# Score and broadcast matmuls of a four-branch decoder trunk on 64 rows of the array, or on 128 rows with zeros

## The chip, the cores and the metric

The kernel runs on one core of one Trainium2 chip. The metric is the device time of one execution in microseconds (us). TensorE (PE in the profile; its weight loads have a row of their own, PEld) multiplies, VectorE (DVE), ScalarE (ACT) and GpSimd (POOL) do the rest, and SyncE (SP) issues the weight transfers.

## The reference, cut to what matters

Two layers, 256 tokens, width 2048. Each layer projects the normed input once and feeds four mixers, whose gated outputs are merged, projected and added to the input. The three matmuls that the change touches come from these lines:

```python
# D, latent attention: 8 heads, key of 128 plain + 64 rotary columns (the rotary key is shared by all heads)
q_full = jnp.concatenate([q[..., :MLA_NOPE], q_rope], axis=-1)
k_full = jnp.concatenate([kv[..., :MLA_NOPE], broadcast(k_rope)], axis=-1)
logits = jnp.einsum('bhqd,bhkd->bhqk', q_blk, k) * scale
# B, forgetting attention (FoX): 16 heads of 64 columns
logits = logits + fq[..., :, None] - log_f_cum[..., None, :]
# A, SSD: 16 heads; decay between two tokens from the cumulative sum of one row per head
seg = a_cum[:, :, :, None] - a_cum[:, :, None, :]
```

## The kernel before, in words

Every large product is computed from split operands: a weight piece of 512 KB comes in by DMA (`fetch`, L152), ACT rounds it to `hi`, DVE forms the remainder `lo`, and PE adds three products (`chunk_a` L163: 512 columns a matmul; `chunk_b` L184: 256 columns). Weight pieces stream through five `raw` buffers and three pairs of `hi`/`lo`. Each layer goes through the in-projections of D, C, A and B, with the mixer of the branch before running in the background: a generator on the list `bg`, advanced by one step (`step`) after each piece. A scheduler of the framework then sets the order of each engine's instructions, so that small matmuls of a mixer stand one by one between the three-product groups of the stream.

The small matmuls of this text are:

- Latent attention, `attention` (L244) with `terms` of D (L498): for each head and each of two query blocks, one matmul of 128 rows on `kn` and one of 64 rows on `krope`, for odd heads on rows 64 to 127 (L257). `S_D` is the PSUM tile of the scores.
- FoX, the same function with `fterms` (L784): per head a bias matmul of 128 rows on `fR` (L254, 384 columns) and two score matmuls of 64 rows on `fk` (L257). `S_B` is the tile. Even heads lie on rows 0 to 63, odd ones on rows 64 to 127.
- SSD, `ssd_gen` (L687): per head one matmul of 64 rows (L721) that spreads the head's row of `aR` over all partitions, into `rb`.

Scores on `krope` and `fk` are plain fp32 and leave two records each, two passes over the columns; the `rb` and `fR` matmuls are in the rounded type of the stream and leave one. The transposes of the probabilities (`pt_B`, `pt_D`, L283) and the products of the GLA branch (`gla_o`, L637) are also plain fp32, on 128 rows.

Of the kernel before, what the change touches and what calls it, by code (L numbers as in the profile page):

```python
# [18 lines left out]
P = 128  # L19
# [18 lines left out]
def trunk(ctx: ExitStack, tc: tile.TileContext, x, pos, vecs, rows, dskip, pre, post, glaw2,  # L38
# [25 lines left out]

# [1 line left out]
    xt = [slot(i, f"x0_{i}") for i in range(2)]  # L66
# [32 lines left out]

# [1 line left out]
    cos = cp.tile([P, T], F32, tag="cos", name="cos")  # L101
# [33 lines left out]

# [1 line left out]
    bg = []  # L137
# [25 lines left out]
    def chunk_a(src, p0, nk, xh, xl, k0, name, groups=None, own=None):  # L163
        """acc[token, 512 columns] over nk row blocks; within a group of pieces the first 128 tokens go first"""
        acc = acc_tile(name)
        a2 = [acc[:, 0], acc[:, 1]]
        if own:
            a2[1] = ps.tile([P, 2, 512], F32, tag="s", name=name + "_1")[:, 0]
        kp = 0
        for n in groups or [1] * (nk // 2):  # L170
            w = [fetch(src[p0 + kp + i], own=own[i] if own and n > 1 else None) for i in range(n)]
            ks = [(2 * kp + i, w[i // 2], slice((i % 2) * 512, (i % 2 + 1) * 512)) for i in range(2 * n)]
            order = ([(tt, k) for k in ks for tt in range(2)] if n == 1 else
                     [(tt, k) for tt in range(2) for k in ks])
            for tt, (k, (hi, lo), c) in order:
                ts_ = slice(tt * P, (tt + 1) * P)
                PE.matmul(a2[tt], xh[:, k0 + k, ts_], hi[:, c], start=(k == 0), stop=False)  # L177
                PE.matmul(a2[tt], xh[:, k0 + k, ts_], lo[:, c], start=False, stop=False)  # L178
                PE.matmul(a2[tt], xl[:, k0 + k, ts_], hi[:, c], start=False, stop=(k == nk - 1))  # L179
            kp += n  # L180
            step(n)
        return a2 if own else acc
# [29 lines left out]
    def transpose_split(src, nb, dh, dl, d0, scale, name):  # L212
        """src(tt, b) -> [P, P] token-major block; dh/dl[:, d0 + b, :] feature-major."""
        for b2 in range(nb // 2):
            pt = psT(f"tr_{name}{b2}").rearrange("p (a t) -> p a t", a=2)
            for j in range(2):
                for tt in range(2):
                    PE.transpose(pt[:, j, tt * P:(tt + 1) * P], src(tt, 2 * b2 + j), ident)
            d = slice(d0 + 2 * b2, d0 + 2 * b2 + 2)
            if scale is None:  # L220
                S.copy(dh[:, d], pt)
                V.tensor_tensor(dl[:, d], pt, dh[:, d].bitcast(F32), ALU.subtract)
            else:
                for j in range(2):
                    S.activation(dh[:, d0 + 2 * b2 + j], pt[:, j], AF.Copy, scale=scale(2 * b2 + j))
                for j in range(2):
                    b = 2 * b2 + j
                    V.scalar_tensor_tensor(dl[:, d0 + b], pt[:, j], scale(b), dh[:, d0 + b].bitcast(F32),
                                           ALU.mult, ALU.subtract)
            yield  # L230
# [7 lines left out]
    def silu_gate(acc, dst, name):  # L238
        """dst = silu(acc), both [P, 2, 512]"""
        S.activation(dst, acc, AF.Sigmoid)  # L240
        V.tensor_tensor(dst, acc, dst, ALU.mult)

# [1 line left out]
    def attention(npair, dv, scale, terms, bias, v, gate, name):  # L244
# [58 lines left out]

# [1 line left out]
    def norm_x(tt, src, dst, ssq, prow):  # L305
        """hh, hl of 128 tokens from src [P, 2048] and the sums of squares of its parts"""
        tot = small([P, 1], f"xtot{tt}")
# [38 lines left out]
    for l in range(DEPTH):  # L346
# [7 lines left out]

# [1 line left out]
        cc = slot(5, "cc").rearrange("p (a b t) -> p a b t", a=2, b=2)  # L356
# [14 lines left out]
        drain()  # L371
# [1 line left out]
        accs = acc_tile("acc_small")[:, 0, :T]  # L373
        for kh in range(2):
            hi, lo = fetch(w_sm[l, kh], 896)
            for k8 in range(8):
# [4 lines left out]
                PE.matmul(accs[:112], lo[:, c], hh[:, k], start=False, stop=(k == 15))  # L381
        krope = small([P, T], "krope", bufs=1)
        krr = small([P, T], "krr", bufs=1)
        for o in (0, 64):
            S.copy(krope[o:o + 64], accs[0:64])
            S.copy(krr[o:o + 32], accs[32:64])
            S.copy(krr[o + 32:o + 64], accs[0:32])
        raw2 = slot(6, "raw2")
        lr, gw2 = raw2[:16, 0:T], raw2[:16, 512:1024]
# [6 lines left out]
        def gates_gen(l=l, krr=krr, krope=krope, lr=lr, gw2=gw2):  # L396
# [17 lines left out]
            yield  # L414
            # cumulative sums: per 128 tokens (SSD), over all (FoX)
            ca, cf, ce = mxz, zz, e
# [18 lines left out]
            V.tensor_tensor(krr, krr, sin, ALU.mult)  # L435
            V.tensor_tensor(krope, krope, krr, ALU.add)
            yield
            # low-rank gate operands: all four products of the halves stacked along the rows
            for dst, src in ((lrs, lr), (gs, gw2)):
# [9 lines left out]
        gs = small([112, 512], "gs", F32R, bufs=1)  # L449
        aR = small([64, T], "aR", F32R, bufs=1)  # L450
        fR = small([P, 3 * P], "fR", F32R, bufs=1)
# [37 lines left out]

        def mla_gen(l=l, qr=qr, qn=qn, kn=kn, dv_=dv_, lgate=lgate, krope=krope, oh=oh, ol=ol):  # L490
            for o, t in ((0, cos), (4, sin)):
                V.tensor_tensor(qr[:, o:o + 4], qr[:, o:o + 4],
                                t.rearrange("p (o n) -> p o n", o=1).to_broadcast([P, 4, T]), ALU.mult)
            V.tensor_tensor(qr[:, 0:4], qr[:, 0:4], qr[:, 4:8], ALU.add)
            yield

            def terms(h):
                s_ = slice(64 * (h % 2), 64 * (h % 2) + 64)  # L498
                return [(qn[:, h], kn[:, h]), (qr[s_, h // 2], krope[s_])]

            yield from attention(4, 128, 192 ** -0.5, terms, None, dv_, lgate, "D")
            noh = st.tile([P, 8, T], F32R, tag="oh", name="oD_h")
            nol = st.tile([P, 8, T], F32R, tag="ol", name="oD_l")
            res["D"] = (noh, nol)
            yield from transpose_split(lambda tt, b: lgate[:, tt, b * P:(b + 1) * P], 8, noh, nol, 0, None, "oD")
# [4 lines left out]

# [1 line left out]
        gqk = slot(5, "gqk").rearrange("p (s h t) -> p s h t", s=2, h=4)  # L512
# [15 lines left out]

# [1 line left out]
        mixed = sl.tile([P, 2, 2048], F32, tag="mixed", name="mixed")  # L530
# [15 lines left out]

# [1 line left out]
        def gla_gen(l=l, gqk=gqk, gv=gv, gg=gg, lrs=lrs, gs=gs):  # L548
# [113 lines left out]

# [1 line left out]
        xsT = slot(3, "xsT").rearrange("p (a t) -> p a t", a=8)  # L664
# [20 lines left out]

# [1 line left out]
        def ssd_gen(l=l, xsT=xsT, bcT=bcT, zg=zg, aR=aR, tokg=tokg):  # L687
# [26 lines left out]
            for g in range(2):  # L714
                yp = ps.tile([P, 2, 512], F32, tag="s", name=f"y{g}")
                late = []
                for hg in range(8):
                    h = 8 * g + hg
                    pr = psT(f"rb{h}")
                    sel = id2[:64, h:h + 1].to_broadcast([64, P])  # L720
                    PE.matmul(pr[:, 0:T], sel, aR, start=True, stop=True)  # L721
# [40 lines left out]

# [1 line left out]
        fq = slot(5, "fq").rearrange("p (a t) -> p a t", a=8)  # L764
        fk = slot(6, "fk").rearrange("p (a t) -> p a t", a=8)
        for dst in (fq, fk):
            for c in range(2):
                acc = chunk_b(w_in[l], nxt(8), 4, hh, hl, "acc_f")
                if c == 0:
                    S.copy(dst[:, 4 * c:4 * c + 4], acc)  # L770
                else:
                    V.tensor_copy(dst[:, 4 * c:4 * c + 4], acc)
        fv = slot(7, "fv").rearrange("p (a b) -> p a b", a=2)
# [9 lines left out]

        def fterms(h, fq=fq, fk=fk):  # L784
            s_ = slice(64 * (h % 2), 64 * (h % 2) + 64)
            return [(fq[s_, h // 2], fk[s_, h // 2])]

# [10 lines left out]

# [1 line left out]
        mh0 = st.tile([P, 8, T], F32R, tag="oh", name="m_h0")  # L800
# [63 lines left out]

# [1 line left out]
def _a(w):  # L866
    """[K, 512 n] -> pieces [n * K / 256, 128, 1024], two blocks of 128 rows by 512 columns each"""
    K, N = w.shape
# [3 lines left out]
def _b(w):  # L872
    """[2048, 128 n] -> pieces [2 n, 128, 1024], eight blocks of 128 rows by 128 columns each"""
    N = w.shape[1]
    return (w.reshape(2, 8, P, N // P, P).transpose(3, 0, 2, 1, 4).reshape(-1, P, 1024))


def _b4(w):
    """[512, 256 n] -> pieces [n, 128, 1024]: two column blocks by four row blocks"""
    N = w.shape[1]  # L880
# [71 lines left out]
```

## Time and profile before

| | |
|---|---|
| median of 3 runs | 2628.51 us (2628.07 to 2629.09) |
| profiled execution: span from first to last instruction | 2626.6 us |
| mean granted clock of TensorE, as a share | 0.997 |
| PE busy | 2594.7 us, 99% |
| DVE, ACT, POOL busy | 58%, 48%, 1% |
| HBM read | 455.02 MB, 175 GB/s over the span |

No other time is listed for the profiled execution than its span; the median stands 1.9 us above it. PE's records end after the next one has begun, so what a matmul costs is read from the starts: from the last matmul of the stream ahead of it to the second one behind it, less the stream's own pace for two.

### The profile page before, as it was taken

What the parts mean: (1) busy time and instruction counts of PE and PEld (TensorE: products, weight loads), DVE (VectorE), ACT (ScalarE), POOL (GpSimd) and SP (SyncE); (2) the same over time, 40 slices, a digit from 0 to 9 for tenths busy, and PEclk for the clock granted to TensorE, in tenths of its full rate; (3) what the DMA queues carried; (4) which work ended last, traced back from release to release, by engine and by line L of the source; (5) the groups of instructions that cost most, each with busy time, mean ns of one, the idle gap of its engine ahead of it and who ended that gap; (6) DMA issues with size and microseconds to landing.
All of it is one profiled execution on the core that took longest, in us unless ns stands there. A gap on an engine that the chain in (4) does not pass through costs nothing.

```text
span 2626.6 us, 34754 instructions
## 1 busy us (share of the span) xinstructions
PE 2594.7 (99%) x13810; PEld 2203.6 (84%) x13810; DVE 1527.4 (58%) x1880; ACT 1247.9 (48%) x1587; POOL 17.4 (1%) x28
## 2 busy tenths in 40 slices
PE   8999999999999999999999999999999999999998
PEld 6898888988899787888878888889888987788887
DVE  6755854676654455555556558546766544555554
ACT  5644544455444444444455445444554444444443
POOL 0000000000000000000000000000000000000000
PEclk9999999999999999999999999999999999999999
DMA  6544545555555554655655445555545555446554
GB/s 227 184 153 143 162 167 185 184 193 168 169 194 176 168 169 141 218 189 182 213 160 185 145 137 176 169 181 183 174 168 184 185 173 169 164 159 206 188 183 153
DMA packets 126722, 461.48 MB, mean 176 GB/s; under 512 B 14656, under 2 KB 15168, under 8 KB 125664
## 3 DMA queue, kind: packets, MB, share of 16 engines
q1 hardware_dynamic: 126144, 459.11, 53.0%
q8 instruction: 108, 1.77, 0.3%
q14 instruction: 54, 0.44, 0.0%
q10 hardware_dynamic: 416, 0.17, 0.0%
HBM read 455.02 MB, written 4.19 MB: 175 GB/s over the span
## 4 chain that ended last, share of the span: by engine, by line
PE 97%; DVE 1%; ACT 1%; issue 0%; DMA 0%; POOL 0%; SPq 0%; DVEq 0%; POOLq 0%; ACTq 0%
PE acc_mC L178 2%; PE acc_f L194 2%; PE acc_f L193 2%; PE acc_f L192 2%; PE acc_mA L177 2%; PE acc_mD L178 2%; PE acc_mA L178 2%; PE acc_mC L177 2%; PE acc_mD L177 2%; PE acc_mA L179 2%; PE acc_mC L179 2%; PE acc_mD L179 2%; PE acc_mB L178 2%; PE acc_mB L177 2%; PE acc_mB L179 2%; PE acc_y L179 2%
## 5 line engine op out<-in xcount | busy, mean ns | idle before, releaser
L157 DVE TENSOR_TENSOR lo<-raw,hi 128x1024 fp32r<-128x1024 f32 x842 | 1027.5, 1222 | 870.6 <-ACT hi L156 869.2
L156 ACT CAST hi<-raw 128x1024 fp32r<-128x1024 f32 x842 | 882.2, 1050 | 1128.2 <-PE acc_f L193 109.7
L194 PE MATMUL acc_f<-hh,lo 128*128 128x256 f32 x512 | 145.1, 283 | 0.0
L193 PE MATMUL acc_f<-hl,hi 128*128 128x256 f32 x512 | 144.9, 283 | 0.0
L192 PE MATMUL acc_f<-hh,hi 128*128 128x256 f32 x512 | 144.9, 283 | 0.0
L194 PE MATMUL acc_x<-hh,lo 128*128 128x256 f32 x384 | 108.8, 283 | 0.0
L193 PE MATMUL acc_x<-hl,hi 128*128 128x256 f32 x384 | 108.7, 283 | 0.0
L192 PE MATMUL acc_x<-hh,hi 128*128 128x256 f32 x384 | 108.7, 283 | 0.0
L178 PE MATMUL acc_mC<-lo,hh 128*128 128x512 f32 x256 | 104.9, 410 | 0.0
L178 PE MATMUL acc_mD<-lo,hh 128*128 128x512 f32 x256 | 103.1, 403 | 0.0
L178 PE MATMUL acc_mA<-lo,hh 128*128 128x512 f32 x256 | 102.5, 400 | 0.0
L177 PE MATMUL acc_mA<-hi,hh 128*128 128x512 f32 x256 | 101.4, 396 | 0.0
L177 PE MATMUL acc_mC<-hi,hh 128*128 128x512 f32 x256 | 100.5, 393 | 0.0
L178 PE MATMUL acc_mB<-lo,hh 128*128 128x512 f32 x256 | 100.2, 391 | 0.0
L179 PE MATMUL acc_mA<-hi,hl 128*128 128x512 f32 x256 | 100.0, 391 | 0.0
L177 PE MATMUL acc_mD<-hi,hh 128*128 128x512 f32 x256 | 100.0, 391 | 0.0
L179 PE MATMUL acc_mD<-hi,hl 128*128 128x512 f32 x256 | 99.8, 390 | 0.0
L179 PE MATMUL acc_mC<-hi,hl 128*128 128x512 f32 x256 | 99.8, 390 | 0.0
L179 PE MATMUL acc_mB<-hi,hl 128*128 128x512 f32 x256 | 99.7, 389 | 0.0
L177 PE MATMUL acc_mB<-hi,hh 128*128 128x512 f32 x256 | 99.6, 389 | 0.0
L192 PEld LDWEIGHTS acc_f<-hh,hi 128*128 128x128 f32 x512 | 98.3, 192 | 0.1
L193 PEld LDWEIGHTS acc_f<-hl,hi 128*128 128x128 f32 x512 | 98.3, 192 | 0.1
(415 smaller groups left out, 6028.3 us busy)
## 6 DMA issues: line engine op xcount, KB each, us to landing
raw<-in_w_in_dram SPq DMA_DIRECT2D x624, 512.0 KB, 3.4
raw<-in_w_br_dram SPq DMA_DIRECT2D x128, 512.0 KB, 3.4
raw<-in_w_out_dram SPq DMA_DIRECT2D x64, 512.0 KB, 3.3
raw<-in_w_ukv_dram SPq DMA_DIRECT2D x16, 512.0 KB, 4.3
raw<-in_w_uq_dram SPq DMA_DIRECT2D x12, 512.0 KB, 3.3
x<-in_x_dram SPq DMA_DIRECT2D x4, 512.0 KB, 5.7
xr<-in_x_dram SPq DMA_DIRECT2D x2, 1024.0 KB, 7.1
pn<-in_post_dram SPq DMA_DIRECT2D x2, 1024.0 KB, 7.4
```

What stands on the lines that cost most here:

```text
L156: S.copy(hi[:, :n], raw[:, :n])
L157: V.tensor_tensor(lo[:, :n], raw[:, :n], hi[:, :n].bitcast(F32), ALU.subtract)
L177: PE.matmul(a2[tt], xh[:, k0 + k, ts_], hi[:, c], start=(k == 0), stop=False)
L178: PE.matmul(a2[tt], xh[:, k0 + k, ts_], lo[:, c], start=False, stop=False)
L179: PE.matmul(a2[tt], xl[:, k0 + k, ts_], hi[:, c], start=False, stop=(k == nk - 1))
L192: PE.matmul(acc[:, b], hi[:, c], xh[:, k], start=(k == 0), stop=False)
L193: PE.matmul(acc[:, b], hi[:, c], xl[:, k], start=False, stop=False)
L194: PE.matmul(acc[:, b], lo[:, c], xh[:, k], start=False, stop=(k == 15))
```

## The change

The rotary key is written into a tile `kr2` with two halves: the rows of the even heads and zeros, and zeros and the rows of the odd heads. `fk` becomes `fk0` and `fk1` in the same manner, `aR` gets 64 more rows of zeros, and the three matmuls use all 128 rows. `krope` and `krr` move into `raw2`, in slot 6. `fk1` takes slot 4, where the row of the next layer's norm (`prow`) is loaded later. The zeros are written by POOL (`kr2` once, `fk0` and `fk1` in each layer) and by DVE (`aR`). Comments are dropped too.

```diff
+    kr2 = cp.tile([P, 2, T], F32, tag="kr2", name="kr2")
+    G.memset(kr2, 0.0)
...
-        krope = small([P, T], "krope", bufs=1)
-        krr = small([P, T], "krr", bufs=1)
+        raw2 = slot(6, "raw2")
+        krope, krr = raw2[:, 1024:1024 + T], raw2[:, 1280:1280 + T]
...
-            V.tensor_tensor(krope, krope, krr, ALU.add)
+            for i in range(2):
+                o = slice(64 * i, 64 * i + 64)
+                V.tensor_tensor(kr2[o, i], krope[o], krr[o], ALU.add)
...
-        aR = small([64, T], "aR", F32R, bufs=1)
+        aR = small([P, T], "aR", F32R, bufs=1)
+        V.memset(aR[64:128].bitcast(F32), 0.0)
...
-                s_ = slice(64 * (h % 2), 64 * (h % 2) + 64)
-                return [(qn[:, h], kn[:, h]), (qr[s_, h // 2], krope[s_])]
+                return [(qn[:, h], kn[:, h]), (qr[:, h // 2], kr2[:, h % 2])]
...
-                    sel = id2[:64, h:h + 1].to_broadcast([64, P])
+                    sel = id2[:, h:h + 1].to_broadcast([P, P])
...
-        fk = slot(6, "fk").rearrange("p (a t) -> p a t", a=8)
-        for dst in (fq, fk):
+        fk0 = slot(6, "fk0").rearrange("p (a t) -> p a t", a=8)
+        fk1 = slot(4, "fk1").rearrange("p (a t) -> p a t", a=8)
+        G.memset(fk0[64:128], 0.0)
+        G.memset(fk1[0:64], 0.0)
+        for i in range(2):
...
+                if i == 1:
+                    S.copy(fk0[0:64, cs], acc[0:64])
+                    V.tensor_copy(fk1[64:128, cs], acc[64:128])
...
-            s_ = slice(64 * (h % 2), 64 * (h % 2) + 64)
-            return [(fq[s_, h // 2], fk[s_, h // 2])]
+            return [(fq[:, h // 2], fk[h % 2][:, h // 2])]
```

PE, the first scores of D in layer 0, before (row counts of the array are not printed; `krope` is the 64-row operand):

```order
L177 MATMUL acc_uv<-hi,cT_h 128x512
L257 MATMUL S_D_1491<-krope,qr 128x128
L257 MATMUL S_D_1491<-kn,qn 128x256
L257 MATMUL S_D_1491<-krope,qr 128x256
L257 MATMUL S_D_1491<-kn,qn 128x128
```

The same place in the changed kernel:

```order
L179 MATMUL acc_uv<-hi,cT_h 128x512
L259 MATMUL S_D_1493<-kr_94,qr 128x128
L259 MATMUL S_D_1493<-kn,qn 128x256
L259 MATMUL S_D_1493<-kr_94,qr 128x256
L259 MATMUL S_D_1493<-kn,qn 128x128
```

Nothing moved: apart from the operand's name all 12883 rows of PE stand in the same order in both kernels.

POOL in layer 0, from the GLA branch (`gn_rs`) to the SSD branch (`sn_rs`) and the output norm, before:

```order
L585 MEMSET gla_a 128x1024
L62 TENSOR_TENSOR gn_rs<-gn_ms,neghalf 128x2 x4
L62 TENSOR_TENSOR sn_rs<-sn_ms,neghalf 128x2 x2
L62 TENSOR_TENSOR yn_rs<-yn_ms,neghalf 128x1 x2
```

The same place in the changed kernel:

```order
L588 MEMSET gla_a 128x1024
L62 TENSOR_TENSOR gn_rs<-gn_ms,neghalf 128x2 x3
L770 MEMSET fk_6057 64x2048
L62 TENSOR_TENSOR gn_rs<-gn_ms,neghalf 128x2
L771 MEMSET fk_6058 64x2048
L62 TENSOR_TENSOR sn_rs<-sn_ms,neghalf 128x2 x2
```

The zeros of `fk0` stand ahead of the GLA branch's last root, those of `fk1` behind it.

SP in the changed kernel, near the end of the first layer's FoX scores (`in_w_br` are the branch output weights):

```order
L156 DMA raw<-in_w_br_dram 128x1024 x4
L336 DMA prow<-in_pre_dram 128x2048
L156 DMA raw<-in_w_in_dram 128x1024 x5
L336 DMA pn<-in_post_dram 128x2048
L156 DMA raw<-in_w_in_dram 128x1024 x3
```

`prow` stood 148 transfers earlier before; now it has to wait for the last matmul that reads `fk1`.

## Rows read from the trace of the kernel before

**Rows 1.** The page, part 1: busy time in us, share of the span and instructions of each engine.

```profile
PE 2594.7 (99%) x13810; PEld 2203.6 (84%) x13810; DVE 1527.4 (58%) x1880; ACT 1247.9 (48%) x1587; POOL 17.4 (1%) x28
```

**Rows 2.** The page, part 4: the chain that ended last, by engine.

```profile
PE 97%; DVE 1%; ACT 1%; issue 0%; DMA 0%; POOL 0%; SPq 0%; DVEq 0%; POOLq 0%; ACTq 0%
```

**Rows 3.** Waits of PE: who waited for whom, us in total, times, longest.

```profile
PE tr_x L319 <- DVE xn L314: 8.9, 1, 8.9
PE tr_x L319 <- DVE y L316: 7.6, 1, 7.6
PE acc_c L177 <- ACT hi L156: 2.8, 1, 2.8
```

**Rows 4.** Timeline of PE, two heads of the SSD broadcast in the z projection: start us, us, engine, line, op, out<-in, rows*columns of the array, moving operand, records.

```profile
574.66 0.39 PE L179 MATMUL acc_z<-hi,hl 128*128 128x512 f32 x1
...
575.57 0.39 PE L177 MATMUL acc_z<-hi,hh 128*128 128x512 f32 x1
575.89 0.50 PE L721 MATMUL rb<-aR,id 64*128 64x256 f32 x2
...
576.65 0.40 PE L179 MATMUL acc_z<-hi,hl 128*128 128x512 f32 x1
```

**Rows 5.** Timeline of the weight loads (PEld) at the same place; idle time before in brackets.

```profile
575.35 0.19 PEld L177 LDWEIGHTS acc_z<-hi,hh 128*128 128x128 f32 x1
575.89 0.29 PEld L721 LDWEIGHTS rb<-aR,id 64*128 64x128 f32 x2 [0.35 <-PE acc_z L179]
```

**Rows 6.** Timeline of PE: one FoX bias matmul, 128 rows, in the fv projection.

```profile
836.53 0.39 PE L177 MATMUL acc_fv<-hi,hh 128*128 128x512 f32 x1
836.75 0.34 PE L254 MATMUL S_B<-fR,id 128*128 128x384 f32 x1
...
837.17 0.39 PE L179 MATMUL acc_fv<-hi,hl 128*128 128x512 f32 x1
```

**Rows 7.** Timeline of PE: one FoX score matmul of 128 columns, and one of 256, 64 rows.

```profile
839.46 0.39 PE L177 MATMUL acc_fv<-hi,hh 128*128 128x512 f32 x1
839.78 0.48 PE L257 MATMUL S_B<-fk,fq 64*128 64x128 f32 x2
...
840.53 0.39 PE L179 MATMUL acc_fv<-hi,hl 128*128 128x512 f32 x1
...
842.82 0.39 PE L177 MATMUL acc_fv<-hi,hh 128*128 128x512 f32 x1
843.14 0.70 PE L257 MATMUL S_B<-fk,fq 64*128 64x256 f32 x2
...
844.10 0.39 PE L179 MATMUL acc_fv<-hi,hl 128*128 128x512 f32 x1
```

**Rows 8.** Timeline of PE: plain fp32 on 128 rows, a transpose of 128 columns and a GLA product of 256.

```profile
855.07 0.40 PE L177 MATMUL acc_fv<-hi,hh 128*128 128x512 f32 x1
855.31 0.38 PE L283 MATMUL pt_B<-ident,pr 128*128 128x128 f32 x2
...
855.76 0.39 PE L179 MATMUL acc_fv<-hi,hl 128*128 128x512 f32 x1
...
1693.11 0.39 PE L177 MATMUL acc_bD<-hi,oD_h 128*128 128x512 f32 x1
1693.34 0.59 PE L637 MATMUL gla_o<-gv,gla_a 128*128 128x256 f32 x2
...
1694.00 0.40 PE L179 MATMUL acc_bD<-hi,oD_l 128*128 128x512 f32 x1
```

**Rows 9.** Timeline of PE: the scores of one pair of D's heads between two matmuls of the gq projection.

```profile
178.40 0.28 PE L193 MATMUL acc_g<-hl,hi 128*128 128x256 f32 x1
...
179.60 0.28 PE L194 MATMUL acc_g<-hh,lo 128*128 128x256 f32 x1
...
180.03 0.48 PE L257 MATMUL S_D<-krope,qr 64*128 64x128 f32 x2
...
184.01 0.28 PE L193 MATMUL acc_g<-hl,hi 128*128 128x256 f32 x1
```

**Rows 10.** Timeline of PE: a head's two scores side by side, the last of layer 0.

```profile
1030.63 0.92 PE L257 MATMUL S_B<-fk,fq 64*128 64x128 f32 x4
```

**Rows 11.** Timeline of POOL: a memset, and the GLA branch's last root of layer 0.

```profile
233.48 0.95 POOL L585 MEMSET gla_a<- 128x1024 f32 x1 [163.96 <-PE o_D L295]
...
399.48 0.70 POOL L62 TENSOR_TENSOR gn_rs<-gn_ms,neghalf 128x2 f32<-128x2 f32 x1 [3.34 <-DVE gn_ms L60]
```

**Rows 12.** The chain of work in order of time: transposes of the GLA branch's output.

```profile
475.64 0.76 PE tr_oC L218 x7
```

**Rows 13.** DVE's copy of the FoX keys out of PSUM: count, ns min/median/max, first and last start.

```profile
L772 DVE COPY fk<-acc_f x2: 1225/1225/1225, 830.2 to 2136.6; 128x1024 f32<-128x1024 f32 x2
```

**Rows 14.** Timeline of SP's queue: four branch weight pieces, and the next ones of the stream.

```profile
1017.46 11.13 SPq L154 DMA_DIRECT2D raw<-in_w_br_dram  x4
1032.51 15.22 SPq L154 DMA_DIRECT2D raw<-in_w_in_dram  x5
```

**Rows 15.** Timelines of ACT and PE: the last exponential of FoX's first pair of heads, and the transpose that reads it.

```profile
850.13 0.48 ACT L274 ACTIVATE pr<-S_B,Bnb 128x256 f32<-128x256 f32 x1
...
852.09 0.60 PE L283 MATMUL pt_B<-ident,pr 128*128 128x128 f32 x4
```

More of the change, by code (lines that the diff above doesn't have):

```diff
@@ L387, in trunk @@
             S.copy(krr[o + 32:o + 64], accs[0:32])
-        raw2 = slot(6, "raw2")
         lr, gw2 = raw2[:16, 0:T], raw2[:16, 512:1024]
@@ L488, in trunk, with mla_gen @@
             S.copy(dv_[:, :, c * 512:(c + 1) * 512], acc)
-        def mla_gen(l=l, qr=qr, qn=qn, kn=kn, dv_=dv_, lgate=lgate, krope=krope, oh=oh, ol=ol):
+        def mla_gen(l=l, qr=qr, qn=qn, kn=kn, dv_=dv_, lgate=lgate, oh=oh, ol=ol):
             for o, t in ((0, cos), (4, sin)):
@@ L764, in trunk @@
         fq = slot(5, "fq").rearrange("p (a t) -> p a t", a=8)
-        fk = slot(6, "fk").rearrange("p (a t) -> p a t", a=8)
-        for dst in (fq, fk):
+        fk0 = slot(6, "fk0").rearrange("p (a t) -> p a t", a=8)
[3 more added lines that the diff above has]
+        for i in range(2):
             for c in range(2):
                 acc = chunk_b(w_in[l], nxt(8), 4, hh, hl, "acc_f")
-                if c == 0:
-                    S.copy(dst[:, 4 * c:4 * c + 4], acc)
+                cs = slice(4 * c, 4 * c + 4)
+                if i == 1:
+                    S.copy(fk0[0:64, cs], acc[0:64])
+                    V.tensor_copy(fk1[64:128, cs], acc[64:128])
+                elif c == 0:
+                    S.copy(fq[:, cs], acc)
                 else:
-                    V.tensor_copy(dst[:, 4 * c:4 * c + 4], acc)
+                    V.tensor_copy(fq[:, cs], acc)
         fv = slot(7, "fv").rearrange("p (a b) -> p a b", a=2)
@@ L782, in trunk, with fterms @@
             silu_gate(acc, fg[:, :, c * 512:(c + 1) * 512], "fg")
-        def fterms(h, fq=fq, fk=fk):
-            s_ = slice(64 * (h % 2), 64 * (h % 2) + 64)
-            return [(fq[s_, h // 2], fk[s_, h // 2])]
+        def fterms(h, fq=fq, fk=(fk0, fk1)):
+            return [(fq[:, h // 2], fk[h % 2][:, h // 2])]
         def fbias(h, fR=fR):
```

## The prediction

> **What bounds the kernel now.** I read the engines' shares first, then the chain that ended last, then PE's waits, then PE's timeline around the three kinds of matmul that change. The shares show PE busy for 99% of the span, DVE and ACT about half [rows 1]; the chain that sets the end is PE for 97% [rows 2]. PE's waits for other engines are few: the three longest are 8.9, 7.6 and 2.8 us, at the start and between the layers [rows 3], in places that the change doesn't touch. So the program lasts as long as PE needs to work through its order, and the question is what each matmul costs PE. A busy PE of 99% doesn't tell that, since records overlap. The starts do: the stream's matmuls of 512 columns follow each other every (575.57 - 574.66) / 4 = 0.2275 us [rows 4], those of 256 columns every (179.60 - 178.40) / 10 = 0.12 us [rows 9]. What a small matmul costs is the way from the last stream matmul ahead of it to the second one behind it, less two such steps.
>
> **What a visit to 64 rows costs.** I call a visit each stretch of 64-row matmuls between 128-row ones.
> - SSD, two `rb` matmuls side by side: 576.65 - 575.57 = 1.08, less 0.455, is 0.625 us [rows 4]. On 128 rows two such passes of 256 columns should cost 2 x 0.12 = 0.24 at the stream's step [rows 9]. The nearest row of the same kind, the FoX bias with the same sort of stationary operand on 128 rows, costs 837.17 - 836.53 - 0.455 = 0.185 for 384 columns [rows 6], which is 0.25 for 512. The visit costs 0.38.
> - FoX, a score of 128 columns: 840.53 - 839.46 - 0.455 = 0.615 [rows 7], against 855.76 - 855.07 - 0.455 = 0.235 for a plain fp32 matmul of 128 columns on 128 rows [rows 8]: 0.38. A score of 256 columns: 844.10 - 842.82 - 0.455 = 0.825 [rows 7], against 1694.00 - 1693.11 - 0.455 = 0.435 for the GLA product of 256 columns [rows 8]: 0.39. So the price hangs on the visit and not on the columns, and not on the number of passes either: `rb` has one pass, a score two.
> - D: a pair of heads has eight scores, four on each row count in turn: 184.01 - 179.60 = 4.41, less two steps of 0.12, is 4.17 [rows 9]. Eight matmuls on 128 rows cost 4 x 0.235 + 4 x 0.435 = 2.68 by rows 8. That leaves 1.49 for four visits, 0.37 each. Matmuls in one chain pay the entry from the stream once and not eight times, so 0.37 is the low end here; with some 0.02 less for each in the chain it is 0.40.
>
> The weight loads show where it goes: the load for `rb` starts 0.35 us after the one before has ended, and only with the matmul, where the stream's loads of 0.19 run one matmul ahead [rows 5].
>
> **How many visits.** From the code, D has 8 heads x 2 query blocks x 2 layers = 32 matmuls on `krope`, each between 128-row neighbours: 32 visits. FoX has 16 x 2 x 2 = 64; on PE's timeline 22 times a head's two scores stand side by side, as in rows 10, which leaves 42 visits. SSD has 32 matmuls, six times two side by side as in rows 4: 26. Together 100.
>
> **The change part by part.**
> - The three matmuls keep their count, columns and place in PE's order, and lose the visits. I take 0.39 us for each, between 0.37 and 0.40: 100 x 0.39 = 39 us, with the ends 37 and 40.
> - The zeros: POOL gets one small memset at the start and two of 64x2048 in each layer. A memset of 1024 columns takes 0.95 [rows 11], so I estimate 1.9 for one. They hold back what POOL has to do behind them. That of `fk0` stands before the GLA branch's last root, at 399.48 [rows 11], and may delay it by up to 1.9; its product is first needed by PE in the transposes at 475.64 [rows 12], 76 us later. I count nothing; uncovered, both layers and both tiles would cost 4 x 1.9 = 7.6 us. POOL is busy for 1% [rows 1], so there is no gain in it either.
> - The FoX keys leave PSUM in halves, ACT's and DVE's for each of the two accumulators, where one engine took each before: one more copy on each engine and layer, as long as the whole one since the columns stay the same, 1.23 us on DVE [rows 13]. Between the copies the weight stream has three pairs of `hi` and `lo` in hand, and both engines have over 40% free [rows 1]. I count nothing; uncovered it is 2 x 1.23 = 2.5 us.
> - The split sum of the rotary key and the zeros of `aR` add short DVE work long before PE reads the result; with the copies' cover I count nothing, and put at most one copy's time, 1.2 us, for each layer.
> - `prow` waits for the last matmul on `fk1`; every weight transfer behind it waits too (below). I count nothing.
>
> Sum: 39 us off PE's path. The profiled span of 2626.6 would become 2587.6; with the 1.9 us by which the median stands above it, **2589.5 us**.
>
> **Two rules of the Trainium skill that speak against the change.** The trace has 128-row loads of 0.19 us that start while the matmul before still runs and leave the stream's step at 0.2275 [rows 4, 5]. The Trainium skill, page "TensorE: Matmul & The Clock Gate", section "Part 3: Packing small matmuls — row/col tiling", says instead that a load overlaps with matmuls under way only where it aims at other row groups. By that rule padding would expose the loads of all padded matmuls. The rows of the stream contradict it, and it stays as the no-change case below. The other is the skill's "TensorEngine Tiling (Array Packing)", section "Theoretical Speedup": up to twice the speed for a contraction of 64 rows or less, from two tiles at work at once. Here a head's two passes of 256 columns take 0.825 on 64 rows and 0.435 on 128 [rows 7, 8], so nothing of such a gain is seen that zeros could lose.
>
> **Rivals.**
> 1. *Only the entry goes.* The first matmul of a visit starts 0.32 after the stream's last one instead of 0.2275 [rows 4], 0.09 late; the rest of the price falls behind it and could belong to the change of operand type. Then 100 x 0.09 = 9 us: 2619.5. Against it: `rb` is of the stream's own type and pays as much as the scores, and `pt_B` and `gla_o` change the type and pay little. 5%.
> 2. *The softmax chain becomes the bound.* The transposes wait for ACT's exponentials; the first one has 852.09 - 850.61 = 1.48 us to spare [rows 15]. If FoX's chain through DVE and ACT were the limit as soon as PE is faster, its 42 x 0.39 = 16.4 would be given back: 2606. Against it: no visit lies between the scores of a pair and their transposes, PE waits for none of them today [rows 3], and the spare is larger than the visits of one pair of heads take on either side of it. 5%.
> 3. *Loads become exposed.* 224 padded records (64 for D, 128 for FoX, 32 for SSD) with a load of 0.19 [rows 5] are 42.6 us, which eats the gain: 2632, no difference that counts. 2%.
> 4. *The array doesn't care for the row count* and the price is that of a small matmul with a rare operand: 2628.5. `fR` at 0.185 speaks against it. 2%.
> 5. *Slower: SP's queue stands still.* `prow` is issued behind the four branch pieces that SP handed out until 1017.46 + 11.13 = 1028.59; it waits for the last score on `fk1`, over at 1030.63 + 0.92 = 1031.55 [rows 10, 14], and the next weight piece went out at 1032.51 anyway. If it had to wait for much later work instead, every weight piece would, and PE would run dry after the five buffers, 5 x 12 matmuls x 0.2275 = 13.7 us of stream. It decides from 39 + 13.7 = 53 us of standstill on; 65 us would give 2640. 2%.
>
> **How the numbers follow.** My forecast has 84%: 2589.5 with an own range of 2588.5 (40 us off) to 2591.5 (37 us off). The uncovered costs of the zeros, copies and sums, 7.6 + 2.5 + 2.4, would put its worst end near 2602; I take two thirds of that, 8.5, for the upper bound, 2598, and go to 2585 below, for visits of 0.43 where a matmul stands alone. Beyond lie the rivals with 16%. Faster by over 0.2% (5 us, about what a measurement can tell here) holds the forecast, rivals 1 and 2: 94%; within it rivals 3 and 4: 4%; slower 2%.
>
> **What would show it.** PE's timeline should show `rb`, `S_D` and `S_B` as 128*128, two `rb` side by side taking 0.24 to 0.25, a lone FoX score 0.235 and 0.435, a pair of D's heads about 2.6 instead of 4.17. Their loads should start ahead of the matmul with no 0.35 of idle time. PE's total wait should stay near today's. I am wrong if the padded matmuls are still followed by a late stream matmul, if PE waits for `pr`, `fk` or POOL, or if the next weight piece behind `prow` comes after 1032 less the time won until then.

## The result, and the profile after

The changed kernel takes 2591.3 us (2591.0 to 2591.7, 4 runs) against 2628.8 us (2628.1 to 2629.1, 4 runs): a ratio of 0.986, with an interval of 0.985 to 0.987. That is 37.5 us less; the forecast was 39 us less and 2589.5 us.

The page of the changed kernel, parts 1 and 4, answers to [rows 1, 2]:

```profile
PE 2558.0 (99%) x13810; PEld 2208.8 (85%) x13810; DVE 1531.6 (59%) x1886; ACT 1248.9 (48%) x1589; POOL 25.1 (1%) x33
PE 98%; ACT 1%; DVE 1%; issue 0%; DMA 0%; POOL 0%; SPq 0%; DVEq 0%; POOLq 0%; ACTq 0%
```

The number of PE's instructions is the same, 13810, and PE is still the chain. POOL's busy time grew by 7.7 us, which are the zeros. The three longest waits of PE in the changed kernel stand at the same places as in [rows 3] and are the same within 0.1 us:

```profile
PE tr_x L321 <- DVE xn L316: 9.0, 1, 9.0
PE tr_x L321 <- DVE y L318: 7.6, 1, 7.6
PE acc_c L179 <- ACT hi L158: 2.7, 1, 2.7
```

So the 37.3 us by which the profiled span shrank (2626.6 to 2589.3) were not idle time of PE. They are in how fast it works through the same order. PE's timeline, two `rb` matmuls side by side, answers to [rows 4]:

```profile
570.04 0.39 PE L179 MATMUL acc_z<-hi,hh 128*128 128x512 f32 x1
570.27 0.40 PE L724 MATMUL rb<-aR,id 128*128 128x256 f32 x2
570.50 0.40 PE L180 MATMUL acc_z<-lo,hh 128*128 128x512 f32 x1
570.74 0.40 PE L181 MATMUL acc_z<-hi,hl 128*128 128x512 f32 x1
```

The `rb` matmuls begin 0.23 us after the stream's last one and not 0.32; the way is 570.74 - 570.04 - 0.455 = 0.245 us where it was 0.625. The matmul that [rows 4] leave out shows where the difference lay:

```profile
576.32 0.50 PE L178 MATMUL acc_z<-lo,hh 128*128 128x512 f32 x1
```

Before, the first `rb` started 0.32 us behind the stream instead of 0.23, the stream's next matmul 0.43 behind that instead of 0.23, and the one after it 0.33 later instead of 0.24: the price lies on the way in and on the way back. The load of `rb` (PEld) starts with the stream's pace, without the idle time of [rows 5]:

```profile
569.82 0.19 PEld L179 LDWEIGHTS acc_z<-hi,hh 128*128 128x128 f32 x1
570.05 0.41 PEld L724 LDWEIGHTS rb<-aR,id 128*128 128x128 f32 x2
```

PE's timeline, a FoX score of 128 and one of 256 columns, answers to [rows 7]:

```profile
828.74 0.39 PE L179 MATMUL acc_fv<-hi,hh 128*128 128x512 f32 x1
828.97 0.38 PE L259 MATMUL S_B<-fk,fq 128*128 128x128 f32 x2
...
829.42 0.40 PE L181 MATMUL acc_fv<-hi,hl 128*128 128x512 f32 x1
...
831.73 0.39 PE L179 MATMUL acc_fv<-hi,hh 128*128 128x512 f32 x1
831.96 0.59 PE L259 MATMUL S_B<-fk,fq 128*128 128x256 f32 x2
...
832.62 0.40 PE L181 MATMUL acc_fv<-hi,hl 128*128 128x512 f32 x1
```

That is 0.225 and 0.435 us, where it was 0.615 and 0.825. And a pair of D's heads, which answers to [rows 9]:

```profile
178.75 0.28 PE L196 MATMUL acc_g<-hh,lo 128*128 128x256 f32 x1
178.87 0.39 PE L259 MATMUL S_D<-kn,qn 128*128 128x128 f32 x2
179.09 0.39 PE L259 MATMUL S_D<-kr,qr 128*128 128x128 f32 x2
...
181.31 0.47 PE L194 MATMUL acc_g<-hh,hi 128*128 128x256 f32 x1
181.61 0.28 PE L195 MATMUL acc_g<-hl,hi 128*128 128x256 f32 x1
```

181.61 - 178.75 - 0.24 is 2.62 us, where it was 4.17.

Since PE's order is the same record for record, the gain can be read place by place: the start of a record before, less the start of the same record after, and how this difference grows over a stage. The stages are given by their time in the kernel before, layer 0; layer 1 adds the same within 0.05 us.

| stage | 64-row stretches in two layers | gain per layer | both | one stretch |
|---|---|---|---|---|
| D's scores, 141 to 245 us | 32 | 6.24 | 12.5 | 0.39 |
| SSD, 507 to 761 us | 26 | 4.80 | 9.6 | 0.37 |
| FoX, 761 to 1155 us | 42 | 8.05 | 16.1 | 0.383 |
| start, and between the layers | 0 | | -0.9 | |

The sum is 38.2 - 0.9 = 37.3 us, the whole of it.

### The profile page after: what moved, and what is told of

Read it like the earlier page. It is cut to its first block, busy times and chain, and to the rows that moved or that the text cites. A ratio compares the mean times of both kernels' runs of the same rounds, so it can differ in the third digit from the quotient of the medians.

```text
span 2589.3 us, 34775 instructions
## 1 busy us (share of the span) xinstructions
PE 2558.0 (99%) x13810; PEld 2208.8 (85%) x13810; DVE 1531.6 (59%) x1886; ACT 1248.9 (48%) x1589; POOL 25.1 (1%) x33
## 4 chain that ended last, share of the span: by engine, by line
PE 98%; ACT 1%; DVE 1%; issue 0%; DMA 0%; POOL 0%; SPq 0%; DVEq 0%; POOLq 0%; ACTq 0%
PE acc_f L196 2%; PE acc_f L195 2%; PE acc_f L194 2%; PE acc_mC L180 2%; PE acc_mD L180 2%; PE acc_mA L180 2%; PE acc_mC L179 2%; PE acc_mA L179 2%; PE acc_mD L179 2%; PE acc_mA L181 2%; PE acc_mC L181 2%; PE acc_mD L181 2%; PE acc_mB L181 2%; PE acc_mB L180 2%; PE acc_mB L179 2%; PE acc_y L181 2%
```

## The experiments

The theory under test: each stretch of 64-row matmuls costs a fixed price of some 0.38 us for leaving the full array and coming back, and nothing else of the change counts. What the hardware does in that time no run shows; the runs test what the price depends on.

**One part alone, three times.** `e1_rb` takes over only the SSD part:

```diff
-        aR = small([64, T], "aR", F32R, bufs=1)
+        aR = small([P, T], "aR", F32R, bufs=1)
+        V.memset(aR[64:128].bitcast(F32), 0.0)
...
-                    sel = id2[:64, h:h + 1].to_broadcast([64, P])
+                    sel = id2[:, h:h + 1].to_broadcast([P, P])
```

> The kernel before with only the SSD broadcast (rb) on 128 rows; PE's order is that of before. Visit theory: each of the 26 stretches of 64-row matmuls that go is worth 0.37 us (the trace of the changed kernel gains 9.6 us over the two SSD stretches), so 9.6 us less: 2619.2 for 2628.8. Rival, the price belongs to small matmuls with plain fp32 in two passes: rb has one pass and nothing would change, 2628.8. Rival, all three must be padded before PE gains: 2628.8 as well. In the timeline two rb side by side cost 0.25 instead of 0.64.

Measured: 2618.6 us against 2629.0, ratio 0.996 (0.995 to 0.998); 4.80 us a layer in the SSD stages, the same as in the whole change. `e2_d` takes over only `kr2`, with its zeros and the split sum:

```diff
+    kr2 = cp.tile([P, 2, T], F32, tag="kr2", name="kr2")
+    G.memset(kr2, 0.0)
...
-                return [(qn[:, h], kn[:, h]), (qr[s_, h // 2], krope[s_])]
+                return [(qn[:, h], kn[:, h]), (qr[:, h // 2], kr2[:, h % 2])]
```

> The kernel before with only the rotary key on 128 rows (kr2), slot 6 holding krope and krr as in the change. Visit theory: 32 stretches at 0.39 us, 12.5 us less: 2616.3. Rival, the price is shared between neighbours of one chain and a chain of eight pays once per pair of heads: 8 pairs at about 0.4, 3 us less: 2625.6. A pair of heads costs 2.62 instead of 4.18 in the timeline by the first, about 3.8 by the second.

Measured: 2616.3 us, ratio 0.995 (0.994 to 0.997); 6.24 us a layer. `e3_fox` takes over only the two key tiles, with their zeros and halved copies:

```diff
+        fk1 = slot(4, "fk1").rearrange("p (a t) -> p a t", a=8)
+        G.memset(fk0[64:128], 0.0)
+        G.memset(fk1[0:64], 0.0)
...
-            return [(fq[s_, h // 2], fk[s_, h // 2])]
+            return [(fq[:, h // 2], fk[h % 2][:, h // 2])]
```

> The kernel before with only the FoX keys on 128 rows (fk0, fk1, their zeros on POOL, the copies in halves and prow in a slot that FoX still reads). Visit theory: 42 stretches at 0.383 us, 16.1 us less: 2612.7. Rival, the zeros, halved copies or the later prow eat part of it: more than 2615, with a wait of PE for fk, POOL or a weight piece in the trace that the kernel before doesn't have. The gains of the three parts should add up to the whole 37.5 within about 1.5.

Measured: 2612.4 us, ratio 0.994 (0.992 to 0.995); 8.06 us a layer. By the records' starts in their own stages the parts add up: 12.5 + 9.6 + 16.1 = 38.2 us, as in the whole. The medians don't add up as well: 10.4, 12.7 and 16.7 us are 39.8 against 37.5, and 1.5 us of difference was the most that had been expected. The profiled spans, 10.0, 11.8 and 16.4 against 37.3, show where such a difference comes from: outside the stages that change, at the start and between the layers, each execution loses or wins up to 0.7 us (below). So the stages show no disturbance of one part by another, and matmuls of one pass (`rb`) gain about as much for a stretch as those of two.

**How many rows make a full array.** `e4_rb96` gives `aR` 96 rows:

```diff
-        aR = small([64, T], "aR", F32R, bufs=1)
+        aR = small([96, T], "aR", F32R, bufs=1)
+        V.memset(aR[64:96].bitcast(F32), 0.0)
...
-                    sel = id2[:64, h:h + 1].to_broadcast([64, P])
+                    sel = id2[:96, h:h + 1].to_broadcast([96, P])
```

`e5_rb32` uses 32, and the low parts of the cumulative sums are left out:

```diff
-                    sel = id2[:64, h:h + 1].to_broadcast([64, P])
-                    PE.matmul(pr[:, 0:T], sel, aR, start=True, stop=True)
+                    sel = id2[:32, h:h + 1].to_broadcast([32, P])
+                    PE.matmul(pr[:, 0:T], sel, aR[0:32], start=True, stop=True)
```

> e1 with 96 rows instead of 128 (32 rows of zeros): only the SSD broadcast is changed against the kernel before. Theory A, the array knows halves and the whole, and 96 rows are the whole: 2618.6 as in e1. Theory B, anything but 128 rows makes the array change over: 2628.8, two rb side by side cost 0.64. The trace of before has matmuls of 112 rows (glz, two of 256 columns in 0.25 us) that speak for A.

> The kernel before with rb on 32 rows instead of 64; the low parts of the cumulative sums (rows 32 to 63 of aR) are left out. PE's order is that of the kernel before. Theory, the price is one of leaving the full array and coming back, whatever the smaller row count: 2629 within 1, two rb side by side 0.625 as before. Rival, the price grows as the rows get fewer: at half as much again 26 x 0.19 = 5 us more, 2634.

Measured: with 96 rows 2619.6 us, ratio 0.996 (0.995 to 0.998), and 4.80 us a layer in the SSD stages, as with 128 (the 1 us by which the median stands above that of `e1_rb` lies outside these stages); with 32 rows 2629.0 us, ratio 1.000 (0.999 to 1.001). PE's timeline with 96 rows:

```profile
576.17 0.39 PE L177 MATMUL acc_z<-hi,hh 128*128 128x512 f32 x1
576.39 0.40 PE L722 MATMUL rb<-aR,id 96*128 96x256 f32 x2
576.63 0.40 PE L178 MATMUL acc_z<-lo,hh 128*128 128x512 f32 x1
576.87 0.40 PE L179 MATMUL acc_z<-hi,hl 128*128 128x512 f32 x1
```

and with 32 rows:

```profile
575.70 0.39 PE L177 MATMUL acc_z<-hi,hh 128*128 128x512 f32 x1
576.02 0.50 PE L721 MATMUL rb<-aR,id 32*128 32x256 f32 x2
576.45 0.50 PE L178 MATMUL acc_z<-lo,hh 128*128 128x512 f32 x1
576.79 0.40 PE L179 MATMUL acc_z<-hi,hl 128*128 128x512 f32 x1
```

The first costs 576.87 - 576.17 - 0.455 = 0.245 us, the second 576.79 - 575.70 - 0.455 = 0.635. So the price doesn't grow as the rows get fewer: of the counts tried, 96 cost as little as 128, and 32 as much as 64.

**The zeros on POOL, four times over.** `e7_zeros4` is the changed kernel with each memset of `fk0` and `fk1` written four times:

```diff
-        G.memset(fk0[64:128], 0.0)
-        G.memset(fk1[0:64], 0.0)
+        for _ in range(4):
+            G.memset(fk0[64:128], 0.0)
+        for _ in range(4):
+            G.memset(fk1[0:64], 0.0)
```

> The changed kernel with each memset of fk0 and fk1 done four times: POOL works some 24 us longer, PE's order is the same. Theory, the zeros are covered by the 76 us until the next transposes of that branch: 2591.3 within 0.5, PE waits as before. Rival, POOL's memsets hold back the GLA branch's last root or DVE's access to SBUF: 12 more memsets of 1.9 us are up to 23 us more, 2592 to 2614, with a wait of PE or DVE for POOL in the trace.

> The changed kernel itself once more, beside e9 on the same chip. Its part gains by the trace were 38.2 us, and 0.9 was lost at the start and between the layers, where PE's step is twice as long for some matmuls. If that loss is by chance, the execution profiled here starts otherwise than the first one and the span moves by up to 1 us; if the new zeros at the start cause it, the stretch up to 141 us is late by 0.7 us again against the kernel before. Time 2591.3 within 0.7.

Measured: 2591.1 us (ratio 0.986, 0.984 to 0.987), and beside it `e8_again`, the changed kernel once more, 2591.0 (0.986, 0.984 to 0.987). POOL's timeline with the fourfold zeros shows what they cost and where they lie:

```profile
392.31 1.81 POOL L771 MEMSET fk<- 64x2048 f32 x1 [2.07 <-ACT hi L158]
394.29 0.69 POOL L62 TENSOR_TENSOR gn_rs<-gn_ms,neghalf 128x2 f32<-128x2 f32 x1 [0.17 <-DVE gn_ms L60]
395.04 5.54 POOL L771 MEMSET fk<- 64x2048 f32 x3
564.62 7.39 POOL L773 MEMSET fk<- 64x2048 f32 x4 [164.04 <-PE cb L711]
647.52 0.69 POOL L62 TENSOR_TENSOR sn_rs<-sn_ms,neghalf 128x2 f32<-128x2 f32 x1 [75.50 <-DVE sn_ms L60]
```

A memset takes 1.81 us (1.9 was the estimate). One of the four of `fk0` stands ahead of the GLA branch's root, as in the changed kernel, and ends before the root's operand is there: the 0.17 us of idle time behind it are a wait for DVE. The other three have moved behind the root. Three more of each add 12 x 1.81 = 21.7 us to POOL in the two layers and nothing to the time: before the next root POOL stands idle for 75.50 us anyway. So the run tests zeros behind the root, and the 0.17 us speak for those ahead of it.

**The two halves at once.** The forecast had set aside a rule of the Trainium skill ("TensorEngine Tiling (Array Packing)", section "Theoretical Speedup") by which two 64-row tiles work at the same time. `e6_pairs` has no zeros at all. It issues the scores of the two heads of a pair in turn, first block, then second block, so that even and odd heads, which lie on different halves of the rows, are neighbours:

```diff
+            if bias is not None:
+                for j in range(2):
+                    sel, r = bias(2 * p + j)
                     PE.matmul(sp[:, j, :3 * P], sel, r, start=True, stop=False)
...
+            for tt in range(2):
+                for i in range(nt):
+                    for j in range(2):
+                        q, k = terms(2 * p + j)[i]
```

> No zeros: the kernel before with the scores of a pair of heads issued in turn, even head on rows 0 to 63, odd head on rows 64 to 127, for each block of queries, so that 64-row matmuls stand side by side; biases of both heads first. By the order D has 18 stretches of 64-row matmuls instead of 32 and FoX 30 instead of 42: 26 fewer. Visit theory, going from one half to the other within a stretch is free but nothing runs at once: 26 x 0.385 = 10 us less, 2618.8. Rival, each change of half costs like a visit: the 96 matmuls are then about as many visits as before or more, 2628.8 to 2637. Rival by the Trainium skill (TensorEngine Tiling (Array Packing), Theoretical Speedup), the halves work at once: the 64-row time of about 30 us halves as well, up to 15 us more off, 2604 to 2610.

Measured: 2607.0 us, ratio 0.992 (0.990 to 0.993), 22 us faster. Of these, 26 stretches fewer (74 left of 100) explain 26 x 0.383 = 10 us. The rest is seen in PE's timeline, a pair of D's heads:

```profile
179.57 0.28 PE L194 MATMUL acc_g<-hh,lo 128*128 128x256 f32 x1
...
180.24 0.49 PE L258 MATMUL S_D<-krope,qr 64*128 64x128 f32 x4
...
181.72 0.70 PE L258 MATMUL S_D<-krope,qr 64*128 64x256 f32 x4
...
182.57 0.28 PE L193 MATMUL acc_g<-hl,hi 128*128 128x256 f32 x1
```

Four 64-row records of 256 columns take 0.70 us, as long as two of them took in [rows 7]: in the trace the records come in twos, 7 ns apart. The pair takes 182.57 - 179.57 - 0.24 = 2.76 us, still 0.14 more than padded: it has two stretches, and two prices of 0.38 are more than the half of the 64-row time (0.64) that it saves.

If halves work at once and the price is one for each stretch, then all four scores of a pair in one stretch should beat the zeros: the time of half the passes saved against one price. `e9_onevisit` pads `rb` alone, keeps `krope` and `fk` as they were, and holds a pair's scores together in the scheduler:

```diff
+            with tc.high_priority():
...
+                    for tt in range(2):
+                        for j in range(2):
+                            score(j, tt, 0, False, tt == 1)
...
+                    for j in range(2):
+                        score(j, 0, 1, False, True)
+                    for j in range(2):
+                        score(j, 1, 1, True, False)
```

> A version that may beat both: rb on 128 rows with zeros, scores of D and FoX on 64 rows without zeros, even and odd head in turn, all four 64-row scores of a pair of heads in one stretch (in D the rotary part of the first block, then that of the second, which opens its own group). The score matmuls are given priority in the scheduler, so they keep together and stand earlier. From e6: halves in turn run at once, and a stretch costs about 0.385. Concurrency theory: against before 100 - 24 = 76 stretches less (29.3 us) and half of the 64-row time of D and FoX (24 pairs x 0.637 = 15.3 us) gone: 44.6 us less, 2584, some 7 us under the changed kernel. Rival, the gain of e6 came from fewer stretches and not from running at once: 24 stretches at 0.385 more than in the changed kernel, 2600. Rival, pairs of heads now follow each other so closely that PE waits for the softmax of the pair before: a wait of PE for S_B or S_D on ACT shows in the trace and the time is over 2591.

> e9_onevisit once more, beside e10_headwise on one chip: 2583 within 1.

Measured: 2582.9 us (2582.4 to 2584.3), ratio 0.983 (0.981 to 0.984), and once more (`e9_again`) 2584.1, 0.983 (0.981 to 0.984), just above the 2583 within 1 that was expected. The changed kernel, timed beside the first of these (`e8_again`, above), is 8 us slower, 0.9856 (0.9842 to 0.9871) against 0.9826 (0.9811 to 0.9840); the eight runs of `e9_onevisit` lie between 2582.4 and 2584.3, the four of `e8_again` between 2590.4 and 2592.7. PE's longest waits stand at the same three places as before, so it doesn't wait for the softmax of the pair before. PE's timeline, a pair of FoX heads with its two biases:

```profile
807.21 0.28 PE L194 MATMUL acc_f<-hh,lo 128*128 128x256 f32 x1
807.33 0.51 PE L258 MATMUL S_B<-fR,id 128*128 128x384 f32 x2
807.76 0.93 PE L251 MATMUL S_B<-fk,fq 64*128 64x128 f32 x8
808.62 0.39 PE L192 MATMUL acc_f<-hh,hi 128*128 128x256 f32 x1
808.84 0.28 PE L193 MATMUL acc_f<-hl,hi 128*128 128x256 f32 x1
```

The eight records of 64 rows cost 808.84 - 807.21 - 0.24 = 1.39, less 2 x 0.185 for the biases by [rows 6], 1.02 us. Padded, the same four scores cost 2 x (0.225 + 0.435) = 1.32. So 0.30 us are won for this pair, of which there are 16. A pair of D in the same kernel:

```profile
180.29 0.28 PE L193 MATMUL acc_g<-hl,hi 128*128 128x256 f32 x1
...
180.94 0.93 PE L251 MATMUL S_D<-krope,qr 64*128 64x128 f32 x8
...
182.88 0.28 PE L192 MATMUL acc_g<-hh,hi 128*128 128x256 f32 x1
```

It takes 182.88 - 180.29 - 0.24 = 2.35 us against 2.62 padded, 0.27 for each of 8. Over all pairs that makes 7.0 us. Read by the starts of the same stream matmuls against `e8_again`, whose profiled span is 8.4 us longer, D's stage wins 1.05 us a layer and FoX's 2.73, together 7.6 us. The rest isn't the scores': the priority moved other small matmuls too (SSD's stage is 0.2 us a layer longer, GLA's in the second layer 0.7 shorter), and 0.5 us lie at the start, between the layers and at the end.

Was it the turn-taking? `e10_headwise` is `e9_onevisit` with the even head's scores first in each stretch and the odd head's behind, in FoX (shown) and in D:

```diff
-                    for tt in range(2):
-                        for j in range(2):
+                    for j in range(2):
+                        for tt in range(2):
                             score(j, tt, 0, False, tt == 1)
```

> As e9_onevisit (24 stretches of 64-row scores, rb padded), the same instructions on PE in the same stretches; only inside a stretch all scores of the even head come first and those of the odd head behind, so that the half of the rows changes once and not after every matmul. Theory A, the halves work at once only where neighbours in the order lie on different halves: the four scores of a pair take 2 x 0.213 + 2 x 0.424 = 1.27 us one after the other instead of 0.64, less at most one pass of 0.107 beside each other where the head changes; 24 x 0.53 to 0.64 is 13 to 15 us over e9_onevisit: 2596 to 2598. Rival B, each half takes its matmuls in its own order and runs ahead by itself: the odd head's start beside the even head's, and the time is that of e9_onevisit, 2583. Rival C, e9_onevisit gains because its scores stand together and not because of the halves: 2583 too, but with the records one after the other.

Measured: 2583.8 us (2582.4 to 2584.2), ratio 0.983 (0.981 to 0.984). This refutes theory A and is rival B's number, and the timeline excludes rival C:

```profile
807.74 0.28 PE L194 MATMUL acc_f<-hh,lo 128*128 128x256 f32 x1
807.86 0.51 PE L258 MATMUL S_B<-fR,id 128*128 128x384 f32 x2
808.30 0.93 PE L251 MATMUL S_B<-fk,fq 64*128 64x128 f32 x8
809.16 0.39 PE L192 MATMUL acc_f<-hh,hi 128*128 128x256 f32 x1
```

The eight records take the same 0.86 us until the stream goes on, though the odd head's four stand behind the even head's four in the order. The trace doesn't print which half a record belongs to, but its columns tell: in the order each head's 256 columns stand behind its own 128, and yet the trace begins with all four records of 128 columns, in twos 13 ns apart, and the four of 256 follow. So the odd head's first scores start beside the even head's first, ahead of three records that stand before them: the two halves work off their own matmuls side by side. In the kernel before full-row matmuls stand between the two heads of a pair.

## Why the prediction was right, point by point

- *PE's order is the bound.* Right: same order, the same longest waits, and the place-by-place gain adds up to the span.
- *A visit costs 0.39 us, whatever its columns and passes.* The mechanism is right: the three parts alone, and 96 and 32 rows, all go by the number of stretches. The size is the step that was off a little: 38.2 / 100 = 0.382 us. D has 0.39 as taken, FoX 0.383, SSD 0.37, where I had rounded up over the 0.38 read for `rb`. The upper end, 0.40, rested on 0.02 us less for each matmul in D's chain, which no row showed: the padded pair takes 2.62 where 2.68 was summed up, under 0.01 for each of eight. The size makes up 0.8 of the 1.7 us by which the span was missed (2587.6 forecast, 2589.3 measured).
- *The other 0.9 us* lie where the change does nothing, and go with TensorE's granted clock. 0.7 is lost before 141 us: the stream's first matmuls run at 0.43 us a step until 19.65 us in the changed kernel, until 17.45 us in the kernel before. The profile's first record of the clock, at the full level (2.4 GHz), begins at 19.97 us and at 17.36 us; for the time ahead of it there is none, and the 1.00 printed there is no reading. Between the layers, where PE has stood idle for 7.6 us, the granted clock reads 0.50 (1.2 GHz), and the stream's step there is 0.43 us too. So the start ran at the lower level, in the changed kernel for longer. Over the 13 profiles, the five whose full clock begins at 19.5 us or later reach the first matmul of `acc_uk` at 133.9 to 134.4 us, the other eight at 133.3 to 133.7; four of these five have no zeros on POOL. The other 0.2 went between the layers: there PE worked at the lower level for 5.6 us in the changed kernel and for 5.1 before, and over the eight profiles with the same order, from 0.4 us lost (6.1 us at the lower level) to 0.7 gained (3.6 us), the loss follows this time. Both change from one execution to the next: `e8_again`, the same program as the changed kernel, lost 0.3 at the start and nothing between the layers, and `e9_again` stands 1.7 us above `e9_onevisit` in the profiled span almost by these two places alone.
- *Zeros, copies and sums cost nothing.* Right. The 0.17 us of waiting ahead of the root and the fourfold zeros behind it show it for POOL. For the halved copies (1.23 us each on DVE, as estimated) and the split sums it follows from the parts: `e2_d` and `e3_fox` contain them and win the full price of their stretches.
- *`prow` is not late.* Right. SP's timeline of the changed kernel, which answers to [rows 14]:

```profile
1013.45 0.33 SPq L336 DMA_DIRECT2D prow<-in_pre_dram  x1
1014.52 0.33 SPq L156 DMA_DIRECT2D raw<-in_w_in_dram  x1
```

The next weight piece went out at 1014.52 instead of 1032.51, 18.0 us earlier, where 6.24 + 4.80 + 8.05 less the 0.7 of the start makes 18.4. By the letter of the forecast's sign that is 0.4 us late: SP waits 2.4 us for the last scores before it issues `prow`. No wait of PE comes of it.
- *Rivals.* Rival 1 (only the entry goes, 0.09 a visit) falls with the 4.80 us a layer of `e1_rb`, 0.37 a visit. Rival 2 (the softmax chain) and rival 5 (SP) would show as new waits of PE, and its longest ones are those of before. Rival 3 (exposed loads) and the rule of the Trainium skill behind it ("TensorE: Matmul & The Clock Gate", section "Part 3: Packing small matmuls — row/col tiling") fall with the loads of `rb`, which start at the stream's pace. Rival 4 (the row count doesn't matter) falls with `e1_rb` and `e4_rb96`.
- *"Nothing of such a gain is seen that zeros could lose."* True of the trace of before, and yet the wrong thing to conclude from it. The Trainium skill, "TensorEngine Tiling (Array Packing)", section "Theoretical Speedup", holds on this chip, with 0.70 us for four records where one half alone needs 0.70 for two. The rows that I weighed it by are of a head whose two passes share a half, so they couldn't show it. It didn't touch the forecast's time, since the kernel before didn't use the halves at once, but the zeros give up some 7 us that gathering the scores wins.

## What to carry to other kernels

Count the stretches of small-row matmuls in a dense full-array stream: each costs some 0.38 us here, whatever was in it, and padding the contraction beyond 64 rows (96 were enough for `rb`) takes that away where the data of one matmul can't be paired. Where two matmuls lie on different halves of the rows, gather as many of both as possible into one stretch instead: here they overlapped in either order where no full-array matmul stood between. Which is better follows from one comparison: half of the 64-row time against the prices of the stretches. A pair of D bears it out both ways: with two stretches it lost 0.14 us against the zeros, with one it won 0.27.

## What the runs showed of the hardware that was not expected

- The halves of the rows don't need alternating matmuls: with four records of the even half ahead of it in the order, the odd half's first one began 13 ns after the first of them; when issued in turn it was 7 ns.
- 96 rows cost no stretch (0.245 us for two `rb`, as with 128), while 32 cost about as much as 64 (0.635 and 0.625).
